# A list scheduler's assumed durations, set to fits of the durations in a trace

## Chip, cores and metric

The kernel runs on one core of one Trainium2 chip. The metric is the device time of one execution in microseconds. The median of three runs before the change is 1693.6 us (1693.36 to 1693.68).

## What is computed

Two transformer blocks on 512 tokens of width 1024, in fp32. The first block has two mixers side by side (gated linear attention with 4 heads, "GLA", and latent softmax attention with 8 heads, "MLA"), an MLP of width 4096 and an embedding gate. The second is a pool mixer, a gated convolutional FFN of width 2816, chunk attention with 16 heads, and a second such FFN:

```
h = h + concat(gla(n), mla(n)) @ w_out              # stage mix
h = h + square(relu(norm(h) @ w_up)) @ w_down       # stage mlp
h = h + (p @ w_proj) * sigmoid(norm(h) @ w_gate+b)  # stage ple
x = x + pool_mixer(norm(x))                         # stage pool
x = x + (silu(conv(n @ Wg)) * (n @ Wv)) @ Wo        # stage ffn0
x = x + chunk_attention(norm(x)) @ w_o              # stage att
x = x + (silu(conv(n @ Wg)) * (n @ Wv)) @ Wo        # stage ffn1
```

## The kernel before, in words

Every large product is split into a high and a low part, and each pair of tiles gets three matmuls (`mm3`, L328). Weights come in units of 128 x 1024. Each unit is split by ScalarE (`wh`) and by VectorE or GpSimd (`wl`, L257). TensorE takes the 512 tokens as moving operand, or 256 columns in the token-major products (`tm`, L359: `pgv`, `paq`). The outputs live in 8 PSUM banks.

**What sets the order of the work.** The instructions of each engine run in the order in which the program issues them, and this order is not written out by hand. The kernel is a set of Python generators ("tasks"). Each yields, before a step, the tiles that the step reads, or a condition. `drive` (L197) picks the next step while the program is built: among the tasks whose tiles are expected to be ready when TensorE gets there, it takes the one with the lowest priority number; if none is ready, the one that is ready first. The main task has the number 9. It issues the large products ("filler" below). The attention and GLA chains have 2 to 4 and evacuations have 0, so they go first whenever they are judged ready:

```
now = self.pace.free["tensor"] + self.SLACK
best = min([(t[0], t) for at, t in able if at <= now], ...)
```

What is "expected" comes from `Pace` (L60). For each issued instruction `note` (L82) works out a cost. The instruction starts when its engine is free and its tiles are ready. The engine is then free again after the cost, and the output counts as ready 0.08 us after that (2.0 us for a DMA). So one number is at once how long the engine is held and how long the result takes. A step that is judged ready too early makes its engine wait with all that is queued behind it. One that is judged ready too late is queued behind work that did not have to be ahead of it.

The same clock decides between engines. `first` (L297) takes the engine that is expected to be done first: VectorE or GpSimd for products and differences in SBUF (`sub`, `mul`, L304 and L309), VectorE or ScalarE for scalings and copies (`scaled`, `copy`, L314 and L321), where `TURN` adds 1.0 us to one side.

In the mix stage the filler is `pg`, `pgv` and then `pw` (the output product). `pw` takes GLA's first two heads and MLA's first two pairs, then GLA's last two heads, and last MLA's pairs 2 and 3, for which all of MLA must be done. MLA goes through 4 pairs of heads with 4 tiles of queries each, one tile at a time (`AHEAD_M` = 1, 1). A tile is: scores `msc`; VectorE memsets, maximum and product `msc`, `mnm`, `mnb`; ScalarE exponentials with a sum, `prob`; VectorE reciprocal `mrs` and scaling `prob`; TensorE transposes `mt`; copies `probT`; TensorE `mo` into a divided array (64 columns). Chunk attention has 8 pairs in the same form (`asc`, `sbias`, `anb`, `prob`, `at`, `probT`, `ao`), with up to 4 tiles under way; its `asc` with `aql` uses 64 rows of the array. Its filler is `paq`, then `pw` in three parts, the last of which needs every pair. At the end of a stage the residual `x` is added up, and the next stage's `xsh`, `xsl`, squares `sq` and their sums `pst` are made.

Of the kernel before, what the change touches and what calls it, by code (L numbers as in the profile page):

```python
# [10 lines left out]
F32R = mybir.dt.float32r  # L11
I32 = mybir.dt.int32
AF = mybir.ActivationFunctionType
OP = mybir.AluOpType
AX = mybir.AxisListType

P = 128
# [42 lines left out]
class Pace:  # L60
    """An estimate of when the engines get to each instruction, from which the order of issue is chosen."""

    def __init__(self):
        self.free = dict.fromkeys(("tensor", "vector", "scalar", "gpsimd", "sync"), 0.0)
        self.ready, self.open, self.banks, self.table = {}, {}, [0.0] * 8, None
        self.mine, self.step = set(), 0

    def allot(self, tile):
        """a bank goes to a tile: the one that was given up first"""
        self.ready[tile.tensor.name] = self.banks.pop(0)  # L70
        self.open[tile.tensor.name] = (0, 0.0)

    def give_up(self, n):
        """the n banks that were read last are given up"""
        for name in sorted(self.open, key=lambda k: self.open[k][0])[-n:]:
            self.banks.append(self.open.pop(name)[1])
# [5 lines left out]
    def note(self, engine, op, args, kw):  # L82
        aps = [x for x in list(args) + list(kw.values()) if hasattr(x, "tensor") and hasattr(x, "free_size")]
        outs = aps[:1] + ([kw["accum_out"]] if kw.get("accum_out") is not None else [])
        ins = aps[1:] + (aps[:1] if op == "copy_predicated" else [])
        n, m = self.size(outs[0]), max([self.size(x) for x in ins], default=0)
        if engine == "tensor":
            if op == "transpose":
                cost = 0.109
            elif ins[0].dtype == F32R:  # L90
                cost = max(0.054, n / 2400)
            else:
                cost = max(0.214, n / 600) * (0.5 if outs[0].shape[0] == 64 else 1)
        elif engine == "vector":
            fast = op in ("tensor_copy", "tensor_scalar") and all(x.space == "SB" or "SB" in str(x.space) for x in aps)
            cost = 0.068 + (m if op == "tensor_reduce" else n) / (1920 if fast else 960)
            if any(n > 1 and x.free_size() == 1 for x in ins):
                cost += 0.063
        elif engine == "scalar":
            cost = 0.09 + n / 1190 + (0.093 if len(outs) > 1 or hasattr(kw.get("scale"), "tensor") else 0)  # L100
        elif engine == "gpsimd":
            cost = 0.23 + 0.165 * n if kw.get("op") == OP.pow else 0.1 + n / (350 if ins else 1400)
        else:
            cost = outs[0].shape[0] * n * 4 / 360e3
        if engine == "scalar":
            f = next((str(x) for x in args if isinstance(x, mybir.ActivationFunctionType)), "")
            if any(f.endswith(x) for x in ("Exp", "Ln", "Sin", "Silu", "Sigmoid")) and f != self.table:
                self.table = f
                cost += 1.28
        needs = ins + [x for x in outs if x.tensor.name not in self.mine or engine != "tensor"]  # L110
        start = max([self.free[engine]] + [self.ready.get(x.tensor.name, 0.0) for x in needs])
        if engine == "tensor":
            self.mine.add(outs[0].tensor.name)
        self.free[engine] = start + cost
        self.step += 1
        if engine != "tensor":
            for x in ins:
                if x.tensor.name in self.open:
                    self.open[x.tensor.name] = (self.step, start + cost + 0.08)
        for x in outs:  # L120
            self.ready[x.tensor.name] = start + cost + (2.0 if engine == "sync" else 0.08)
# [22 lines left out]
class Norm:  # L144
    """the residual times a norm's gain, split, and the reciprocal rms: a column per token tile, and broadcast"""
# [15 lines left out]
class Block:  # L161
# [22 lines left out]
    # order of issue ---------------------------------------------------------  # L184
    def spawn(self, gen, prio):
        """gen yields before each step what the step reads, or a condition it waits for"""
# [34 lines left out]
    # memory -------------------------------------------------------------------  # L221
# [24 lines left out]
    # weights --------------------------------------------------------------------  # L246
# [10 lines left out]
    def split_unit(self):  # L257
        """the next unit's high and low parts"""
# [24 lines left out]
    def unit(self, *shape):  # L283
        """the next unit, as (high, low) of [128, blocks, columns]; its split is issued when it is used up"""
# [12 lines left out]
    def first(self, aps, **cost):  # L297
        """the engine that is expected to be done first; cost: fixed part, per element, handicap"""
# [5 lines left out]
    def sub(self, out, a, b):  # L304
        """a - b, all in SBUF"""
        e = self.first((out, a, b), vector=(0.07, 1 / 960, 0), gpsimd=(0.1, 1 / 430, self.HELP))
        getattr(self.nc, e).tensor_sub(out, a, b)

    def mul(self, out, a, b):  # L309
        """a * b, all in SBUF"""  # L310
        e = self.first((out, a, b), vector=(0.07, 1 / 960, 0), gpsimd=(0.1, 1 / 430, self.HELP))
        getattr(self.nc, e).tensor_mul(out, a, b)

    def scaled(self, out, src, col):  # L314
        """src times a column, in SBUF"""
        if self.first((out, src, col), vector=(0.13, 1 / 1920, 0), scalar=(0.18, 1 / 1190, self.TURN)) == "vector":
# [4 lines left out]
    def copy(self, out, ps):  # L321
        """out of PSUM"""
        if self.first((out, ps), vector=(0.07, 1 / 960, self.TURN), scalar=(0.09, 1 / 1190, 0)) == "vector":
# [27 lines left out]
    def fm(self, ps, unit, acts, at=0, n=None):  # L351
        """feature-major product: the unit's blocks from `at` on stationary, acts[k] moving"""
# [6 lines left out]
    def tm(self, xs, out):  # L359
        """token-major product of 256 columns; out: two banks of two token tiles"""  # L360
# [14 lines left out]
    # norms of the residual ------------------------------------------------------  # L375
# [61 lines left out]
    # first block: both mixers ---------------------------------------------------  # L437
# [9 lines left out]
    def mix_start(self, norm):  # L447
        """the first loads in the order of need"""
# [28 lines left out]
        # constants of this part  # L477
# [65 lines left out]
    def latent(self, i, ps, norm):  # L543
        """evacuates latent i (keys and values, queries, queries) or the low-rank gate and rotary key"""
# [37 lines left out]
    def mla_weights(self):  # L582
        """the up-projections' weights, split: [(hi, lo)] of 512 (keys, values) and 384 columns"""
# [7 lines left out]
    def rotate(self, out, src, tab, j, n):  # L591
        """out, src: [P, n, 32]; the two halves of a rotary pair, gains folded into the tables"""
# [13 lines left out]
    def mla(self, norm):  # L606
# [5 lines left out]
        # the shared rotary key  # L612
# [17 lines left out]
        # keys and values  # L630
# [90 lines left out]
    def attend(self, pr, vals, scale, bias, name, ahead, scored):  # L721
        """heads[pr][head]: the products that make up a head's scores; adds the pair's output, transposed and split"""
# [82 lines left out]
    def gla_inputs(self, norm, ft):  # L805
        """queries and keys of two heads, feature-major"""
# [22 lines left out]
    def gla_values(self, norm, ft):  # L829
        """values and output gate of two heads: tiles of two token tiles by two heads"""  # L830
# [19 lines left out]
    def gla_gate(self):  # L850
        """the logarithms of the decays, split: tiles of two token tiles"""
# [31 lines left out]
        # queries of a level, one head's beside the other's with zeros between  # L883
# [5 lines left out]
    def gla(self, ft):  # L889
        """two heads"""  # L890
# [81 lines left out]
        def finish(b, ou):  # L972
            """two token tiles: the heads' norm, the gate, and the result transposed and split"""
# [84 lines left out]
    def part_out(self, acts, after=lambda m: None):  # L1058
        """adds the product of some K tiles with their rows of an output matrix"""
# [61 lines left out]
    # first block: MLP -------------------------------------------------------------  # L1121
# [23 lines left out]
    def product(self, norm, name, finish):  # L1145
        """one feature tile of a product with the normed residual"""
# [8 lines left out]
    def products(self, norm, name, finish, first):  # L1155
        """feature tiles of products with the normed residual; the first two side by side while the residual comes in"""
# [46 lines left out]
    # first block: per-layer embedding gate ------------------------------------------  # L1203
# [14 lines left out]
    def project(self):  # L1218
        """the embedding's projection, which needs nothing of the residual"""
# [43 lines left out]
    # second block: pool mixer ---------------------------------------------------------  # L1263
# [70 lines left out]
    # second block: gated convolutional FFN ----------------------------------------------  # L1334
# [50 lines left out]
    # second block: chunk attention --------------------------------------------------------  # L1385
# [8 lines left out]
    def attention(self, norm, after):  # L1394
# [6 lines left out]
        def heads():  # L1401
            for pr in range(8):
# [3 lines left out]
                # a head's product with both parts of the keys in one pass: the high part of its queries is there twice  # L1406
# [94 lines left out]
    # -----------------------------------------------------------------------------------  # L1501
# [60 lines left out]
def pack_fm(w, kts):  # L1562
    """[K, M] -> one unit per M tile: [128, len(kts) * 128]"""
# [5 lines left out]
def pack_tm(w, n=512, ks=2):  # L1569
    """[K, N] -> units of ks K tiles by n columns, K within a column group first"""  # L1570
# [5 lines left out]
def pack_parts(w, parts):  # L1576
    """[K, M] -> for each group of K tiles, units of 8 blocks: M tiles, and the K tiles of each"""
# [120 lines left out]
```

## Time and profile before

| | |
|---|---|
| median of the runs | 1693.6 us (1693.36 to 1693.68) |
| span of the profiled execution | 1689.6 us |
| between the span and the median, what lies around the span | 4.0 us |
| TensorE busy | 98% of the span |
| VectorE, ScalarE, GpSimd busy | 60%, 43%, 11% |
| mean granted TensorE clock | 0.998 |

The profiled execution has no time of its own beside its span; the three runs lie within 0.32 us, so it is set beside their median. "Busy" is the union of the instructions' intervals. An interval of a matmul goes on after the next one has started, so a busy TensorE is not one that starts matmuls at its full rate. All engine instructions carry line L133 (the wrapper that notes each one), so they are told apart by the names of their tiles.

### The profile page before, as it was taken

What the parts mean: (1) busy time and instruction counts of PE and PEld (TensorE: products, weight loads), DVE (VectorE), ACT (ScalarE), POOL (GpSimd) and SP (SyncE); (2) the same over time, 40 slices, a digit from 0 to 9 for tenths busy, and PEclk for the clock granted to TensorE, in tenths of its full rate; (3) what the DMA queues carried; (4) which work ended last, traced back from release to release, by engine and by line L of the source; (5) the groups of instructions that cost most, each with busy time, mean ns of one, the idle gap of its engine ahead of it and who ended that gap; (6) DMA issues with size and microseconds to landing.
All of it is one profiled execution on the core that took longest, in us unless ns stands there. A gap on an engine that the chain in (4) does not pass through costs nothing.

```text
span 1689.6 us, 22483 instructions
## 1 busy us (share of the span) xinstructions
PE 1660.7 (98%) x8696; PEld 1389.8 (82%) x8696; DVE 1007.0 (60%) x1889; ACT 728.3 (43%) x1422; POOL 184.3 (11%) x190
## 2 busy tenths in 40 slices
PE   8999999999999999999999999999999999999999
PEld 6878777888888888888888888989987788888887
DVE  6986867443444357766644645375768776644642
ACT  6745445432333254643332324365656543322321
POOL 3431302000000012200000001121222100000000
PEclk9999999999999999999999999999999999999999
DMA  6102032333323333233333233312221233333332
GB/s 215 62 26 64 24 115 75 100 100 94 105 88 113 92 90 108 65 109 91 99 100 89 94 100 102 116 64 88 68 96 51 76 100 99 100 102 98 90 100 73
DMA packets 47501, 153.73 MB, mean 91 GB/s; under 512 B 5521, under 2 KB 7458, under 8 KB 47394
## 3 DMA queue, kind: packets, MB, share of 16 engines
q1 hardware_dynamic: 47394, 152.30, 29.2%
q8 instruction: 68, 1.11, 0.3%
q14 instruction: 39, 0.32, 0.1%
HBM read 150.18 MB, written 2.10 MB: 90 GB/s over the span
## 4 chain that ended last, share of the span: by engine, by line
PE 87%; DVE 8%; ACT 3%; issue 1%; DMA 0%; SPq 0%; POOL 0%; DVEq 0%; ACTq 0%
PE pf L133 27%; PE pdn L133 24%; PE pup L133 10%; PE paq L133 7%; PE pw L133 3%; PE pgv L133 2%; PE pgt L133 2%; DVE wl L133 1%; PE pl L133 1%; PE ao L133 1%; PE at L133 1%; ACT aqh L133 1%; DVE xsl L133 1%; PE pg L133 1%; DVE x L133 1%
## 5 line engine op out<-in xcount | busy, mean ns | idle before, releaser
L133 ACT ACTIVATE wh<-ws 128x512 fp32r<-128x512 f32 (+1 forms) x536 | 302.7, 614 | 254.1 <-PE pdn L133 213.9
L133 DVE TENSOR_TENSOR wl<-ws,wh 128x512 fp32r<-128x512 f32 (+1 forms) x508 | 343.8, 717 | 110.6 <-ACT wh L133 110.3
L133 PE MATMUL pf<-xsl,wh 128*128 128x512 f32 x704 | 274.7, 390 | 1.4 <-DVE xsl L133 1.2
L133 PE MATMUL pf<-xsh,wh 128*128 128x512 f32 x704 | 275.4, 391 | 0.0
L133 PE MATMUL pf<-xsh,wl 128*128 128x512 f32 x704 | 274.2, 390 | 0.0
L133 DVE TENSOR_TENSOR x<-x,pdn 128x512 f32<-128x512 f32 (+1 forms) x81 | 55.1, 681 | 219.2 <-PE pdn L133 219.2
L133 PEld LDWEIGHTS pf<-xsl,wh 128*128 128x128 f32 x704 | 132.2, 188 | 31.2 <-DVE xsl L133 3.6
L133 PEld LDWEIGHTS pf<-xsh,wh 128*128 128x128 f32 x704 | 132.2, 188 | 28.2 <-issue 0.5
L133 PEld LDWEIGHTS pf<-xsh,wl 128*128 128x128 f32 x704 | 132.2, 188 | 27.0
L133 PE MATMUL pdn<-yl,wh 128*128 128x512 f32 x352 | 137.1, 389 | 0.0
L133 PE MATMUL pdn<-yh,wl 128*128 128x512 f32 x352 | 137.1, 389 | 0.0
L133 PE MATMUL pdn<-yh,wh 128*128 128x512 f32 x352 | 137.0, 389 | 0.0
L133 POOL TENSOR_TENSOR sq<-sq 128x512 f32<-128x512 f32 x37 | 51.9, 1403 | 744.5 <-ACT sq L133 743.7
L133 PE MATMUL paq<-wh,xsh 128*128 128x256 f32 x384 | 113.2, 295 | 0.8 <-DVE aql L133 0.4
L133 PE MATMUL paq<-wh,xsl 128*128 128x256 f32 x384 | 109.4, 285 | 0.0
L133 PE MATMUL paq<-wl,xsh 128*128 128x256 f32 x384 | 109.4, 285 | 0.0
L133 PE MATMUL pup<-xsl,wh 128*128 128x512 f32 x256 | 99.8, 390 | 0.4 <-DVE xsl L133 0.4
L133 PE MATMUL pup<-xsh,wh 128*128 128x512 f32 x256 | 100.2, 391 | 0.0
L133 PE MATMUL pup<-xsh,wl 128*128 128x512 f32 x256 | 99.7, 389 | 0.0
L133 PE MATMUL pdn<-hl,wh 128*128 128x512 f32 x256 | 99.7, 389 | 0.0
L133 PE MATMUL pdn<-hh,wl 128*128 128x512 f32 x256 | 99.7, 389 | 0.0
L133 PE MATMUL pdn<-hh,wh 128*128 128x512 f32 x256 | 99.7, 389 | 0.0
(292 smaller groups left out, 3092.3 us busy)
## 6 DMA issues: line engine op xcount, KB each, us to landing
ws<-in_w_fg SPq DMA_DIRECT2D x44, 512.0 KB, 3.6
ws<-in_w_fv SPq DMA_DIRECT2D x44, 512.0 KB, 3.6
ws<-in_w_up SPq DMA_DIRECT2D x32, 512.0 KB, 3.6
ws<-in_w_down SPq DMA_DIRECT2D x32, 512.0 KB, 3.6
ws<-in_w_fo SPq DMA_DIRECT2D x32, 448.0 KB, 3.2
ws<-in_w_fo SPq DMA_DIRECT2D x16, 512.0 KB, 3.6
ws<-in_w_out SPq DMA_DIRECT2D x8, 512.0 KB, 3.6
ws<-in_w_gate SPq DMA_DIRECT2D x8, 512.0 KB, 3.7
```

What stands on the lines that cost most here:

```text
L133: return call(*args, **kw)
```

## The change

The costs in `Pace.note` and the engines' prices in `sub`, `mul`, `scaled` and `copy` are replaced. `Pace` gets one more state, `mode`, the part of the array that the last matmul used; a matmul in another mode is charged 0.1 us more (coming from the whole array) or 0.2 us more (coming from a divided one), and one with 64 rows or 64 columns costs half. The kernel's instructions, their sizes and data, the tasks, their priorities and the other constants stay as they are; docstrings and comments are dropped.

```diff
         if engine == "tensor":
+            rows, columns = ins[0].shape[0], self.size(ins[0])
             if op == "transpose":
-                cost = 0.109
-            elif ins[0].dtype == F32R:
-                cost = max(0.054, n / 2400)
+                cost, mode = 0.109, (P, P)
             else:
-                cost = max(0.214, n / 600) * (0.5 if outs[0].shape[0] == 64 else 1)
+                mode = tuple(next(t for t in (32, 64, P) if x <= t) for x in (rows, columns))
+                cost = n / 2400 + 0.0135 if ins[0].dtype == F32R else max(0.224, n / 600 + 0.005)
+                if 64 in mode:
+                    cost *= 0.5
+            if mode != self.mode:
+                cost += 0.1 if self.mode == (P, P) else 0.2
+                self.mode = mode
         elif engine == "vector":
             fast = op in ("tensor_copy", "tensor_scalar") and all(...)
-            cost = 0.068 + (m if op == "tensor_reduce" else n) / (1920 if fast else 960)
+            cost = 0.152 + (m if op == "tensor_reduce" else n) / (1920 if fast else 960)
             if any(n > 1 and x.free_size() == 1 for x in ins):
-                cost += 0.063
+                cost += 0.065
         elif engine == "scalar":
-            cost = 0.09 + n / 1190 + (0.093 if len(outs) > 1 or hasattr(kw.get("scale"), "tensor") else 0)
+            cost = 0.165 + n / 1190 + (0.19 if len(outs) > 1 else 0)
+            cost += 0.1 * sum(hasattr(kw.get(x), "tensor") for x in ("scale", "bias"))
         elif engine == "gpsimd":
-            cost = 0.23 + 0.165 * n if kw.get("op") == OP.pow else 0.1 + n / (350 if ins else 1400)
+            cost = 0.38 + 0.157 * n if kw.get("op") == OP.pow else 0.175 + n / (459 if ins else 1400)
...
     def sub(self, out, a, b):          # and mul
-        e = self.first((out, a, b), vector=(0.07, 1 / 960, 0), gpsimd=(0.1, 1 / 430, self.HELP))
+        e = self.first((out, a, b), vector=(0.152, 1 / 960, 0), gpsimd=(0.175, 1 / 459, self.HELP))
...
-        if self.first((out, src, col), vector=(0.13, 1 / 1920, 0), scalar=(0.18, 1 / 1190, self.TURN)) == "vector":
+        if self.first((out, src, col), vector=(0.217, 1 / 1920, 0), scalar=(0.265, 1 / 1190, self.TURN)) == "vector":
...
-        if self.first((out, ps), vector=(0.07, 1 / 960, self.TURN), scalar=(0.09, 1 / 1190, 0)) == "vector":
+        if self.first((out, ps), vector=(0.152, 1 / 960, self.TURN), scalar=(0.165, 1 / 1190, 0)) == "vector":
```

## Rows read from the trace of the kernel before

**Rows 1.** The page: span, engines, the chain that ended last by engine.

```profile
span 1689.6 us, 22483 instructions
PE 1660.7 (98%) x8696; PEld 1389.8 (82%) x8696; DVE 1007.0 (60%) x1889; ACT 728.3 (43%) x1422; POOL 184.3 (11%) x190
...
PE 87%; DVE 8%; ACT 3%; issue 1%; DMA 0%; SPq 0%; POOL 0%; DVEq 0%; ACTq 0%
```

**Rows 2.** Busy time by stretch: engine busy us (x instructions), then clock, DMA share, GB/s.

```profile
72.00:203.00 131.00, 124.41 (x901) 105.21 (x900) 102.00 (x304) 65.50 (x156) 43.21 (x70) 1.00 0.14 41
203.00:253.00 50.00, 49.54 (x271) 38.00 (x269) 34.38 (x90) 27.12 (x64) 2.46 (x2) 1.00 0.33 106
253.00:276.00 23.00, 20.65 (x91) 16.20 (x90) 20.26 (x25) 13.24 (x23) 7.59 (x5) 1.00 0.22 68
276.00:618.00 342.00, 342.00 (x1510) 283.05 (x1510) 154.22 (x237) 119.41 (x207) 7.54 (x6) 1.00 0.33 98
...
714.00:1058.00 344.00, 344.00 (x1520) 285.00 (x1519) 196.87 (x293) 124.38 (x213) 9.27 (x8) 1.00 0.33 99
1058.00:1311.00 253.00, 248.75 (x1972) 223.73 (x1972) 168.45 (x365) 144.48 (x348) 51.66 (x48) 0.99 0.24 78
```

**Rows 3.** The chain of waits in order of time: start us, us, what.

```profile
238.18 1.06 PE msc L133 x4
239.24 4.78 PE pw L133 x21
244.02 0.44 PE mt L133 x4
...
251.88 0.17 PE mt L133
...
862.17 43.52 PE pdn L133 x192
```

**Rows 4.** Waits of TensorE from 40 to 254 us: sum, times, longest.

```profile
PE mt L133 <- DVE prob L133: 1.7, 2, 1.5
PE pe L133 <- DVE sct L133: 1.6, 3, 0.8
PE po L133 <- DVE msc L133: 1.1, 2, 0.6
```

**Rows 5.** Waits of TensorE from 254 us to the end, same columns.

```profile
PE pst L133 <- DVE sq L133: 3.2, 3, 1.7
PE at L133 <- DVE prob L133: 2.5, 2, 1.5
```

**Rows 6.** Timeline of VectorE, 238 to 252 us: one MLA tile's instructions.

```profile
240.21 1.28 DVE L133 TENSOR_TENSOR x<-x,pw 128x512 f32<-128x512 f32 x2
242.02 0.69 DVE L133 TENSOR_TENSOR x<-x,pw 128x512 f32<-128x512 f32 x1 [0.53 <-PE pw L133]
242.62 0.16 DVE L133 RECIPROCAL mrs<-msu 128x2 f32<-128x2 f32 x1
242.82 0.62 DVE L133 TENSOR_SCALAR prob<-prob,mrs 128x256 f32<-128x256 f32 x2
```

**Rows 7.** Timeline of ScalarE in the same tile.

```profile
240.79 0.19 ACT L133 ACTIVATION_READ_ACCUMULATOR prob<-msc,mnb,qs 128x1 f32 x1
240.88 0.56 ACT L133 ACTIVATE prob<-msc,mnb,qs 128x256 f32<-128x256 f32 x1
241.33 0.20 ACT L133 ACTIVATION_READ_ACCUMULATOR prob<-msc,mnb,qs 128x1 f32 x1
```

**Rows 8.** Timeline of TensorE, 1307 to 1312 us: the last tiles of chunk attention.

```profile
1310.56 0.40 PE L133 MATMUL pw<-omh,wl 128*128 128x512 f32 x1
1310.89 0.44 PE L133 MATMUL ao<-probT,aqkv 128*64 128x128 f32 x4
```

**Rows 9.** VectorE and GpSimd lines, 0 to 276 us: count, busy us, mean ns.

```profile
L133 DVE TENSOR_TENSOR wl<-ws,wh 128x512 fp32r<-128x512 f32 (+1 forms) x52 | 40.1, 812 | 15.9 <-ACT wh L133 15.7
L133 POOL TENSOR_TENSOR wl<-ws,wh 128x512 fp32r<-128x512 f32 x4 | 5.2, 1320 | 6.2 <-ACT wh L133 6.1
```

More of the change, by code (lines that the diff above doesn't have):

```diff
@@ L65, in __init__ @@
         self.ready, self.open, self.banks, self.table = {}, {}, [0.0] * 8, None
-        self.mine, self.step = set(), 0
+        self.mine, self.step, self.mode = set(), 0, (P, P)
     def allot(self, tile):
@@ L304, in sub @@
     def sub(self, out, a, b):
-        e = self.first((out, a, b), vector=(0.07, 1 / 960, 0), gpsimd=(0.1, 1 / 430, self.HELP))
+        e = self.first((out, a, b), vector=(0.152, 1 / 960, 0), gpsimd=(0.175, 1 / 459, self.HELP))
         getattr(self.nc, e).tensor_sub(out, a, b)
     def mul(self, out, a, b):
-        e = self.first((out, a, b), vector=(0.07, 1 / 960, 0), gpsimd=(0.1, 1 / 430, self.HELP))
+        e = self.first((out, a, b), vector=(0.152, 1 / 960, 0), gpsimd=(0.175, 1 / 459, self.HELP))
         getattr(self.nc, e).tensor_mul(out, a, b)
     def scaled(self, out, src, col):
-        if self.first((out, src, col), vector=(0.13, 1 / 1920, 0), scalar=(0.18, 1 / 1190, self.TURN)) == "vector":
+        if self.first((out, src, col), vector=(0.217, 1 / 1920, 0), scalar=(0.265, 1 / 1190, self.TURN)) == "vector":
             self.nc.vector.tensor_scalar(out, src, col, None, op0=OP.mult)
```

## Prediction

> **What bounds the kernel now.** I read the page first: TensorE is busy for 98% of the span and carries 87% of the chain that ended last [rows 1]. The reader is to see that little is left to gain by order alone. The table of stretches says where. In 276 to 618 us and 714 to 1058 us TensorE is busy for the whole stretch [rows 2], and the chain of waits shows the rate there: 192 matmuls of 512 columns in 43.52 us [rows 3], 0.2267 us each. No order of the other engines changes that, so these stretches (and ffn1 after 1334 us, of the same make) count as zero. TensorE has idle time only where attention and GLA steps are mixed into the filler: 131.00 - 124.41 = 6.6 us in 72 to 203, 0.5 in 203 to 253, 2.3 in 253 to 276, and 253.00 - 248.75 = 4.3 in 1058 to 1311 [rows 2]. Together that is 13.7 us. The lists of TensorE's waits say for whom: nearly all for VectorE, on a chain's step that was issued before its data were there (`prob`, `sct`, `msc`, and `sq` ahead of the sums `pst`) [rows 4, 5]. While it waits, filler stands behind it in the queue. So the planner of before is too optimistic at these places, and its costs can move at most these idle times, and whatever a new order adds.
>
> **How far the old costs are off.** TensorE: n/2400 gives 0.2133 us for 512 columns, the trace 0.2267 [rows 3]. The planner's TensorE runs 6% fast, and the new cost gives 0.2268. VectorE: one add of 512 elements lasts 0.69 us, but two back to back take 1.28 us, so the second starts 0.59 us after the first [rows 6]. The old cost 0.068 + 512/960 = 0.601 is the time for which the engine is held; with the 0.08 us that follow, the result comes after 0.68 us, which is the duration. The new cost is the duration, 0.685, so engine and result are each late, by 0.084 us. ScalarE: an exponential of 256 columns with its sum holds the engine 0.45 + 0.09 = 0.54 us (starts at 240.79, 240.88 and 241.33) [rows 7]. The old cost is 0.09 + 0.215 + 0.093 = 0.40, the new one 0.165 + 0.215 + 0.19 + 0.2 = 0.77. So TensorE's fit becomes right, VectorE's goes from right to 14% too long for 512 elements (and to twice as long for the smallest), and ScalarE's goes from too short to too long.
>
> **The change part by part.**
>
> *Instructions.* None is added or removed, the DMAs too are the same; only their order on each engine and the choice between engines move. The dividing term saves no switch: `drive` chooses by priority and readiness, not by cost. It only makes the planner's TensorE later at `mo`, `ao` and `aql`. Zero by itself.
>
> *TensorE's waits.* For an MLA tile of 256 columns I add the planner's costs from the last score to the first transpose (2 memsets, 2 maxima, a product, 2 exponentials, a reciprocal, 2 scalings, with the 0.08 us at each hand-over). Old: 0.27 + 0.67 + 0.15 + 0.88 + 0.15 + 0.61 + 0.08 = 2.8 us. New: 0.44 + 0.84 + 0.23 + 1.62 + 0.23 + 0.78 + 0.08 = 4.2 us. So the transposes are placed 1.4 us later by the planner's clock, less what its slower TensorE takes back: a tile's period is about 9 us, 6% of that is 0.5 us. About 0.9 us net, four of the new filler matmuls more between scores and transposes. Of the listed waits three are longer than 1.2 us (1.5, 1.5, 1.7) [rows 4, 5]; the others would be covered by 0.9 us of filler, and these shortened. The sums `pst` come after VectorE's `xsl` and `sq`, all dearer by 0.084 us, and have the next stage's filler to stand behind. Bounds: nothing is gained, if the new order makes as many waits as it takes away; all 13.7 us go but for 0.7 (the first products that wait for `xsl` or `oml` and have nothing else to run), and each wait gives back 0.39 - 0.23 = 0.16 us of a pipeline that ran empty, some 16 times 2.6 us: 15.6. I take **-8**, near the middle, because 0.9 us covers most of the single waits, while VectorE's queue has a new order too and will be late at places of its own.
>
> *VectorE's own blocks.* In the tile at 240 us the reciprocal stood behind an add of `x` that waited 0.53 us for `pw` [rows 6]; the planner had thought TensorE further on. The right matmul cost takes this away. It is part of what the chains gain, and I count it in the next term.
>
> *The ends of the chains.* MLA's 16 tiles come one after another. The last transposes are at 251.88 us, and the filler before the last part of `pw` ran until then [rows 3]; in chunk attention the last `ao` follows three filler matmuls [rows 8]. At both ends chain and filler run out together, so a later chain shows as an idle TensorE. With 0.9 us a tile, 16 tiles are 14 us late against the filler, which is 1.5 tiles of 9 us; each of them left without filler costs at most the 4.78 us between its scores and transposes and some 1.4 us between those and `mo` [rows 3], 9 us in all. It costs nothing if the chain's lost waits (7.1 us of idle time until 253 us) and blocks bring it forward as much. Chunk attention has four tiles under way, which hides lateness until the last pair: 0 to 4 us. I take **+4** of these 13 for both, since the last tiles are the smallest and have an empty VectorE before them (34.38 of 50 us) [rows 2].
>
> *Choice of engine.* The price gap of a 512-element difference between GpSimd and VectorE falls from 1.29 - 0.60 = 0.69 to 1.29 - 0.685 = 0.61 us, and the planner's VectorE is further behind, so more `wl` go to GpSimd than the 4 beside 52 until 276 us [rows 9]. That relieves VectorE by 0.6 us each; but `wl` takes 812 ns there on average [rows 9] against 690 for an add of the same size [rows 6], so something slows it, and more work on GpSimd may slow it more. Bounds -2 and +3, taken as **0**.
>
> Sum: -8 + 4 + 0 = -4. The profiled execution has span 1689.6 us [rows 1], and 4.0 us lie around it to the median 1693.6, to which the runs keep within 0.2 us. I predict **1689.6 us**.
>
> **The rivals.** About 0.2%, 3.4 us, is what a measurement of this kernel can tell from no change.
>
> *Slower: the planner's VectorE is full.* From 72 to 203 us VectorE has 304 instructions and is busy for 102.0 us [rows 2]. At 0.084 us more each the planner's VectorE needs up to 127.5 of 131 us. A queue that is nearly full grows, and every chain step behind it is placed late, though the real engine is free. Then the filler is used up with more than two tiles of queries to come, and TensorE idles for the chains at the ends: +9 in mix, +4 in attention, and of the waits only 3 us are saved: +10, 1703.6 us. For it: the start-to-start times above, and ends without margin. Against it: the tile at 238 us took 4.8 us from scores to transposes [rows 3], more than the 4.2 of the new costs. It decides from two tiles left over. The Trainium skill speaks for this rival ("Perfetto Trace Analysis", section "Per-engine timelines"): the interval that the profiler shows for a VectorE or ScalarE instruction ends with the acknowledgement of its last write, and the next one can begin before that. By that rule durations are the wrong thing to hold an engine for, and the time would be this rival's; the trace agrees, with 0.59 us to the next start beside 0.69.
>
> *No change.* New waits replace the old ones, or the ends take back what the waits give: 1690.2 to 1697.0, about 1693. For it: at both ends chain and filler already meet, so the chains themselves, not the waits, may set the length.
>
> *More is gained.* All waits go and the ends keep up: -15.6 + 2, about 1680. For it: the waits sit where the planner's error for TensorE accumulates; against it: VectorE's queue becomes less true, not more.
>
> **How the numbers follow.** Forecast (-3.5 to -9) 0.34, more gained 0.10, no change 0.23, slower 0.33. So faster 0.44, same 0.23, slower 0.33. Range: below, the forecast's waits almost all gone, 1682; above, the slower rival with GpSimd's +3, 1706. Outside lie some of "more gained" and of a worse tail, 0.2 together. The faster cases alone would span 1678 to 1690.
>
> **What would show it.** Right: the dense stretches keep 43.52 us for 192 matmuls; TensorE's waits for `prob`, `sct` and `sq` from 40 us on shrink to about half; the last `mo` before the last part of `pw` comes earlier than 252 us; more `wl` on GpSimd. Wrong: TensorE waits for `prob` or `probT` several times in a row just before the last part of `pw`, in mix or in attention, with no filler between (the slower rival); or a list of waits as long as before at other steps (no change). The forecast falls if the idle time of 72 to 276 us does not shrink.

## The result: 1.0% slower, and the profile after

The changed kernel takes **1711.3 us** (median of four runs, 1708.1 to 1712.0) against 1693.5 us for the kernel before (four runs, 1691.7 to 1693.7): a ratio of 1.0100, with a 95% interval of 1.0085 to 1.0116. The forecast was 1689.6 us, the range ended at 1706. It went the way of the slower rival, and further than that rival's 1703.6.

The page of the changed kernel, lines as in [rows 1]:

```profile
span 1709.0 us, 22482 instructions
PE 1662.7 (97%) x8696; PEld 1390.6 (81%) x8696; DVE 1005.2 (59%) x1852; ACT 730.6 (43%) x1423; POOL 205.5 (12%) x226
...
PE 87%; DVE 9%; ACT 3%; issue 1%; DMA 0%; SPq 0%; DVEq 0%; ACTq 0%
```

The spans differ by 19.4 us. TensorE is busy for only 2.0 us more (1662.7 against 1660.7), so 17.4 us are idle time: 46.3 us instead of 28.9. Where it arose is read from busy time by stretch, with both kernels cut at the same steps: the first down product `pdn` of the MLP, the first and the last `paq` of chunk attention, the end. The columns are those of [rows 2]. First the kernel before, then the changed one:

```profile
0.00:356.20 356.20, 338.10 (x1915) 276.74 (x1916) 254.28 (x644) 189.29 (x389) 83.17 (x104) 1.00 0.27 85
356.20:1057.80 701.60, 700.00 (x3165) 581.10 (x3164) 376.87 (x564) 265.58 (x464) 38.78 (x30) 1.00 0.32 97
1057.80:1257.70 199.90, 197.10 (x1665) 184.22 (x1665) 123.43 (x272) 113.92 (x274) 39.81 (x39) 0.99 0.26 83
1257.70:1689.60 431.90, 425.46 (x1957) 347.76 (x1955) 252.46 (x409) 159.53 (x297) 22.60 (x18) 1.00 0.29 89
```

```profile
0.00:366.90 366.90, 336.42 (x1914) 277.70 (x1915) 252.16 (x612) 188.59 (x389) 99.74 (x136) 0.99 0.25 83
366.90:1071.80 704.90, 700.77 (x3165) 581.19 (x3164) 374.65 (x561) 267.14 (x466) 39.23 (x31) 1.00 0.31 97
1071.80:1277.30 205.50, 199.61 (x1664) 183.55 (x1664) 125.29 (x273) 115.29 (x273) 40.36 (x39) 0.99 0.25 80
1277.30:1709.00 431.70, 425.94 (x1957) 348.12 (x1955) 253.14 (x406) 159.61 (x296) 26.17 (x20) 1.00 0.29 89
```

The loss is 10.7 us up to the MLP's first down product, 3.3 in the middle, 5.6 in `paq`, and -0.2 after that. In the first stretch TensorE's idle time grew from 18.1 to 30.5 us, though VectorE has 2.1 us less to do. TensorE's longest waits, as in [rows 4, 5] but over the whole span:

```profile
PE pl L139 <- ACT wh L139: 9.5, 1, 9.5
PE mt L139 <- DVE prob L139: 5.6, 3, 3.0
PE at L139 <- DVE prob L139: 4.6, 5, 1.1
PE po L139 <- DVE sct L139: 3.9, 2, 2.6
PE pf L139 <- DVE xsl L139: 3.1, 2, 2.3
PE plv L139 <- DVE gqt L139: 2.3, 1, 2.3
```

The first is the wait for the first weights. It had 7.8 us before, and the runs below that keep the changed kernel's order have 8.1 and 8.3, so more than 1 of the 10.7 us is scatter of the start and not the order's. Of the others, `mt` for `prob` had 1.7 us before, `at` for `prob` 2.5. Only the wait of the sums `pst` for `sq` shrank as forecast, from 3.2 to 0.4 us.

**MLA's chain starts late.** All its scores, first in the kernel before, then in the changed one (shortest, median and longest duration in ns, then the first and the last start in us):

```profile
L133 PE MATMUL msc<-hd x64: 273/484/595, 75.2 to 247.5; 96*128 96x512 f32 x16, 96*128 96x384 f32 x16, 96*128 96x256 f32 x16, 96*128 96x128 f32 x16
L139 PE MATMUL msc<-hd x64: 273/484/676, 90.8 to 260.4; 96*128 96x512 f32 x16, 96*128 96x384 f32 x16, 96*128 96x256 f32 x16, 96*128 96x128 f32 x16
```

The first scores come 15.6 us later, and the last group of `mo` 11.6 us later (263.96 for 252.39). From the one to the other the changed kernel takes 4 us less, so the chain is late from its start and not by a little more in each tile.

**The end of mix.** The chain of waits of the changed kernel, 242 to 260 us (start, length, what):

```profile
242.45 1.49 PE msc L139 x4
243.94 7.50 PE pw L139 x33
251.44 0.66 PE mt L139 x6
...
253.60 1.07 PE msc L139 x4
```

And TensorE's timeline right behind it:

```profile
257.63 0.76 PE L139 MATMUL mt<-ident,prob 128*128 128x128 f32 x4 [2.97 <-DVE prob L139]
...
263.12 0.69 PE L139 MATMUL mt<-ident,prob 128*128 128x128 f32 x2 [2.33 <-DVE prob L139]
263.96 0.90 PE L139 MATMUL mo<-probT,vm 128*64 128x128 f32 x4 [0.15 <-ACT probT L139]
264.79 0.80 PE L139 MATMUL pw<-omh,wh 128*128 128x512 f32 x1
```

The filler between scores and transposes of the last three tiles was, in the kernel before:

```profile
230.56 4.79 PE pw L133 x21
...
239.24 4.78 PE pw L133 x21
...
247.78 4.10 PE pw L133 x18
```

Here the first of these three tiles got 33, three more stand ahead of its `mo`, and then the filler was used up: the last two tiles have none, and TensorE waits 2.97 and 2.33 us. The last part of `pw` starts at 264.79 instead of 253.0 us. VectorE's timeline shows what stood ahead of the tile with 33:

```profile
245.21 1.87 DVE L139 TENSOR_TENSOR x<-x,pw 128x512 f32<-128x512 f32 x3
247.30 1.29 DVE L139 TENSOR_TENSOR wl<-ws,wh 128x512 fp32r<-128x512 f32 x2 [0.21 <-ACT wh L139]
248.51 0.68 DVE L139 TENSOR_TENSOR x<-x,pw 128x512 f32<-128x512 f32 x1
249.11 0.16 DVE L139 RECIPROCAL mrs<-msu 128x2 f32<-128x2 f32 x1
```

The row sums were there at 246.75 us, but the reciprocal stands in VectorE's order behind four additions and two `wl`. In the program its step is picked only when the planner expects the sums, so it presumably expected ScalarE's exponentials later than they were; the planner's clock is in no trace, so this is not shown.

**The clock.** Behind the first of those two waits TensorE lost some of its clock. The same view by stretch, around them:

```profile
253.00:259.00 6.00, 2.88 (x24) 1.76 (x22) 2.32 (x9) 1.92 (x6) 0.00 (x0) 1.00 0.00 0
259.00:270.00 11.00, 8.52 (x29) 6.21 (x30) 4.70 (x13) 4.36 (x11) 0.00 (x0) 0.53 0.14 44
```

And for two single microseconds of it:

```profile
258.00:259.00 1.00, 0.85 (x7) 0.48 (x8) 0.00 (x0) 0.71 (x2) 0.00 (x0) 1.00 0.00 0
259.00:260.00 1.00, 1.00 (x8) 0.71 (x9) 0.00 (x0) 0.00 (x0) 0.00 (x0) 0.64 0.00 0
```

TensorE was busy for 2.88 of 6 us, and in the 11 us that follow the mean granted clock is 0.53, mostly the lower level of 1.2 GHz. It fell between 259 and 260 us, behind the first wait and ahead of the second. The 48 matmuls of the last part of `pw` took 13.0 us (264.8 to 277.8, from the first start to the last). At the rate of [rows 3] that would be 10.7, so the clock cost some 2.3 us there. Before, the same part took 11.4 us at full clock, some 0.7 of it lost around a wait for `oml`.

### The profile page after: what moved, and what is told of

Its sections match the earlier page's. It is cut to its first block, busy times and chain, and to the rows that moved or that the text cites. A ratio compares the mean times of both kernels' runs of the same rounds, so it can differ in the third digit from the quotient of the medians.

```text
span 1709.0 us, 22482 instructions
## 1 busy us (share of the span) xinstructions
PE 1662.7 (97%) x8696; PEld 1390.6 (81%) x8696; DVE 1005.2 (59%) x1852; ACT 730.6 (43%) x1423; POOL 205.5 (12%) x226
## 4 chain that ended last, share of the span: by engine, by line
PE 87%; DVE 9%; ACT 3%; issue 1%; DMA 0%; SPq 0%; DVEq 0%; ACTq 0%
PE pf L139 27%; PE pdn L139 24%; PE pup L139 10%; PE paq L139 6%; PE pw L139 4%; PE pgt L139 3%; PE pgv L139 2%; PE pl L139 1%; PE ao L139 1%; DVE gqt L139 1%; PE at L139 1%; PE msc L139 1%; ACT aqh L139 1%; DVE prob L139 1%; DVE wl L139 1%
## 5 line engine op out<-in xcount | busy, mean ns | idle before, releaser
L139 DVE TENSOR_TENSOR wl<-ws,wh 128x512 fp32r<-128x512 f32 (+1 forms) x497 | 335.5, 715 | 129.2 <-ACT wh L139 129.1
```

The lines of the kernel that those rows point to most:

```text
L139: return call(*args, **kw)
```

## Experiments

Ratios are to runs of the kernel before on the same chip in the same session, with 95% intervals.

### One part of the change at a time

The kernel before, with TensorE's costs alone:

```diff
+rows, columns = ins[0].shape[0], self.size(ins[0])
...
+    cost = n / 2400 + 0.0135 if ins[0].dtype == F32R else ...
...
+if mode != self.mode: ...
```

> Only TensorE's costs of the change, with the term for a divided array; VectorE, ScalarE, GpSimd and the prices as before. Theory A (the harm is in charging a VectorE or ScalarE instruction its whole duration as time for which the engine is held): no slower than before, 1685 to 1695 us, MLA's first scores near 75 us as before. Theory B (TensorE's new costs or the term for the divided array move the filler wrongly): most of the 18 us are here, 1703 to 1713. Theory C (any new order loses some microseconds against the old one, whatever its costs): 1696 to 1705.

1715.5 us, ratio 1.0132 (1.0114 to 1.0151). So the one fit that became true [rows 3], together with the term for the divided array, loses by itself, and more than any of the three theories had. TensorE waits for `sq` twice for 3.3 us and once 3.6 us for `xsl`.

VectorE's costs alone:

```diff
-cost = 0.068 + ...
+cost = 0.152 + ...
```

> Only VectorE's costs of the change in the planner's clock. Theory A: VectorE is overbooked in the planner, MLA's chain starts late (first scores after 85 us instead of 75) and its last tiles have no filler: 1700 to 1712 us. Theory B: within 3 us of before. Theory C: 1696 to 1705.

1711.4 us, 1.0105 (1.0085 to 1.0126): as much as the whole change, and where Theory A had it. MLA's first scores come at 89.6 us, as late as in the whole change, and the last tile has no filler. The longest wait is one `po` for `mrs`, 4.8 us.

```profile
L133 PE MATMUL msc<-hd x64: 272/484/736, 89.6 to 266.2; 96*128 96x512 f32 x16, 96*128 96x384 f32 x16, 96*128 96x256 f32 x16, 96*128 96x128 f32 x16
```

ScalarE's costs alone:

```diff
-cost = 0.09 + n / 1190 + (0.093 if ...)
+cost = 0.165 + n / 1190 + (0.19 if len(outs) > 1 else 0)
+cost += 0.1 * sum(...)
```

> Only ScalarE's costs of the change in the planner's clock. Theory A: MLA's chain starts as before (75 us), since VectorE and TensorE set that, but each tile's exponentials are placed late, the filler is gone before the last tiles, and TensorE waits for them at the end of mix: 1697 to 1708 us. Theory B: within 3 us of before. Theory C: 1696 to 1705.

1729.9 us, 1.0228 (1.0204 to 1.0252), the worst part. What Theory A described came, with the first scores at 78.4 us, but the time is 22 us above its range. TensorE's timeline shows the end of mix without filler for four tiles, not two:

```profile
266.64 1.97 PE L134 MATMUL mt<-ident,prob 128*128 128x128 f32 x8 [2.93 <-DVE prob L134]
...
277.63 1.51 PE L134 MATMUL mt<-ident,prob 128*128 128x128 f32 x6 [3.50 <-DVE prob L134]
...
286.05 0.96 PE L134 MATMUL mt<-ident,prob 128*128 128x128 f32 x4 [2.96 <-DVE prob L134]
...
292.16 0.43 PE L134 MATMUL mt<-ident,prob 128*128 128x128 f32 x2 [2.42 <-DVE prob L134]
```

GpSimd's costs and the prices in `first` alone:

```diff
-cost = ... 0.1 + n / (350 if ins else 1400)
+cost = ... 0.175 + n / (459 if ins else 1400)
...
-vector=(0.07, 1 / 960, 0), gpsimd=(0.1, 1 / 430, self.HELP)
+vector=(0.152, 1 / 960, 0), gpsimd=(0.175, 1 / 459, self.HELP)
```

> Only GpSimd's costs and the prices between engines (sub, mul, scaled, copy). Theory A: GpSimd's fit is nearer to its start-to-start times than the old one, so no harm, 1688 to 1696 us. Theory B: within 3 us of before. Theory C: 1696 to 1705.

1708.4 us, 1.0095 (1.0071 to 1.0120), above all three theories. Each part alone loses 15 to 37 us, 92 in sum where the whole loses 18. So the parts don't add up, and no part is the cause by itself. MLA's late start does belong to one part: with TensorE's, ScalarE's or GpSimd's costs alone the first scores come at 77.9 to 78.6 us, with VectorE's alone at 89.6. But an end of mix without filler is not the only way to lose: with TensorE's or GpSimd's costs alone each of the last three tiles has 15 to 21 filler matmuls behind its scores, and in the profiled executions the first `pdn` still comes at 370.3 and 372.3 us instead of 356.2.

### Is any other order worse?

Three shifts of the old costs that mean next to nothing, and one repair of the change: its costs for TensorE and GpSimd, VectorE and ScalarE held from start to start, their results handed over later (this last diff is against the changed kernel).

```diff
-SLACK = -0.1
+SLACK = -0.15
```

> The kernel before with every old cost; only the constant SLACK of the planner is -0.15 us instead of -0.1, a change that makes no cost truer or less true. Theory C (the old order is one picked among many that the old costs and constants can give, and any other order loses): 1700 to 1712 us. Theory A (only wrong holding times lose): within 4 us of before.

```diff
-cost = max(0.054, n / 2400)
+cost = max(0.054, n / 2388)
```

> The kernel before, with the F32R matmul's cost n/2388 in place of n/2400, half a percent more and so a little truer. Theory C: 1700 to 1712 us. Theory A: within 4 us of before.

```diff
-cost = 0.068 + ...
+cost = 0.070 + ...
```

> The kernel before, with VectorE's fixed cost 0.070 us in place of 0.068. Theory C: 1700 to 1712 us. Theory A: within 4 us of before.

```diff
-cost = 0.152 + ...
+cost = 0.068 + ...
...
-cost = 0.165 + n / 1190 + (0.19 ...)
-cost += 0.1 * sum(...)
+cost = 0.09 + n / 1190 + (0.093 ...)
+cost += 0.07 * sum(...)
...
-self.ready[...] = start + cost + (2.0 if engine == "sync" else 0.08)
+self.ready[...] = start + cost + dict(sync=2.0, vector=0.124, scalar=0.135).get(engine, 0.08)
```

> TensorE's and GpSimd's costs and the prices of the change; VectorE and ScalarE are held for the times from one start to the next (the old costs, with the sum at 0.093 us and each column operand of ScalarE at 0.07 us), and their results come 0.124 and 0.135 us after that. This is the planner whose clock is nearest to the trace. Theory A: it beats the change by 10 us or more and is at or below before, 1680 to 1695 us. Theory C: like any new order, 1700 to 1712 us.

Slack: 1693.8 us, 1.0003 (0.9992 to 1.0015). Half a percent on the matmuls: 1701.3, 1.0057 (1.0035 to 1.0079). Two ns on VectorE: 1697.9, 1.0042 (1.0028 to 1.0057). Start-to-start holding: 1705.2, 1.0068 (1.0048 to 1.0089). So 2 ns in one cost can move the time by 0.4%, by nothing but another order, and the repair gains 6 us on the change, but not on the kernel before. Theory A, that only wrong holding times lose, is out: the repair lies 10 us above its range, and half a percent more on the matmuls loses too, though it is nearer to the trace. Theory C, that any other order loses, has the time of these two runs; the shift of the slack lost nothing, and the one of 2 ns lies between the theories.

### Can the change be repaired, and what do shifts of it give?

In the changed kernel: less work for GpSimd, less slack, more slack, 2 ns.

```diff
-HELP, TURN = 0.0, 1.0
+HELP, TURN = 1.0, 1.0
```

> The change with HELP = 1.0 in place of 0: GpSimd gets a difference or product only where the planner has VectorE over 1 us later. Theory E (work moved to GpSimd stretches VectorE's instructions beside it, and so delays the chains): the time falls, 1697 to 1706 us. Theory F (the chains are late because the planner's VectorE is overbooked): VectorE is booked even more, the chains come later still, 1711 to 1725 us.

```diff
-SLACK = -0.1
+SLACK = -0.15
```

> The change with SLACK = -0.15 in place of -0.1, which makes no cost truer or less true. If the 18 us come from the costs, it stays near the change: 1706 to 1716 us. If they come from the picked order of before alone, it may land anywhere between 1695 and 1725 us.

```diff
-SLACK = -0.1
+SLACK = 0.9
```

> The change with SLACK = +0.9: a step counts as ready 1 us earlier against TensorE than in the change. Theory F: about what the new costs put on a tile is taken back, MLA's last tile is done long before the filler ends, TensorE's waits at the end of mix go, 1695 to 1704 us. If the late chains were not the cause: 1708 to 1718 us, or slower by waits of TensorE on steps that are issued too early.

```diff
-cost = 0.152 + ...
+cost = 0.154 + ...
```

> The change with VectorE's fixed cost 0.154 us in place of 0.152. As with the changed SLACK: 1706 to 1716 us if the level belongs to the costs, anywhere between 1695 and 1725 us if orders differ by chance alone.

All are slower than the change: 1731.5 us (1.0213; 1.0195 to 1.0231), 1725.2 (1.0174; 1.0157 to 1.0190), 1733.3 (1.0221; 1.0203 to 1.0240) and 1730.6 (1.0206; 1.0184 to 1.0227). The repairs (less GpSimd, chains let in 1 us earlier) failed. Their times lie above the ranges expected of them, of which the highest ended at 1725 us; only the run with more slack had "or slower" beside its range. The two shifts that mean nothing add 14 and 19 us (13 and 18 by the ratios), so the change itself was a good draw among the orders of its costs that ran.

### Carried on, or lost stage by stage?

The new costs in mix alone, and after mix alone (`self.new` chooses the set, and flips when a stage's generator ends):

```diff
+    self.pace.new = False      # starts True
```

> The new costs hold for the first stage (mix) alone; from its end on the old ones are used. The order on TensorE is that of the changed kernel for its first 1064 rows. Theory G (each stage loses by its own order): mix ends as in the changed kernel, so the first down product starts at 366 to 368 us, and from there on the kernel before repeats itself: its 1329.3 us from that point, so 1700 to 1707 us in all. Theory H (the loss is made in mix and carried on, whatever the later costs): 1709 to 1713 us.

```diff
+    self.pace.new = True       # starts False
```

> The old costs hold in mix, the new ones from its end on. The order on TensorE is that of the kernel before for its first 1053 rows. Theory G: the first down product starts at 356 us as before, and the later stages lose 6 to 10 us by their own order (chunk attention most), 1699 to 1705 us. Theory H: 1692 to 1696 us.

1705.0 us, 1.0061 (1.0044 to 1.0079), and 1702.4, 1.0053 (1.0033 to 1.0074). Above the kernel before (1695.3 in that session) that is 9.7 and 7.1 us, 16.8 in sum, beside the 17.8 of the whole change: Theory G (each stage loses by its own order). Busy time by stretch, cut at the same steps, shows it without the median. New costs in mix alone:

```profile
0.00:367.80 367.80, 339.85 (x1914) 281.36 (x1915) 251.86 (x613) 188.95 (x389) 98.16 (x135) 0.97 0.25 83
367.80:1069.50 701.70, 700.10 (x3165) 581.03 (x3164) 376.65 (x564) 265.38 (x464) 38.93 (x30) 1.00 0.31 97
1069.50:1267.60 198.10, 195.48 (x1664) 182.60 (x1663) 123.30 (x272) 113.91 (x274) 39.97 (x38) 1.00 0.26 83
```

New costs after mix alone:

```profile
0.00:360.10 360.10, 341.45 (x1915) 278.99 (x1916) 254.08 (x644) 189.45 (x389) 83.16 (x104) 0.99 0.26 84
360.10:1065.00 704.90, 700.78 (x3166) 581.24 (x3165) 374.65 (x561) 267.07 (x466) 39.27 (x31) 1.00 0.31 97
1065.00:1269.00 204.00, 198.10 (x1665) 182.12 (x1664) 125.17 (x273) 115.43 (x273) 40.35 (x39) 1.00 0.25 80
```

Each stretch has the length that belongs to its costs: 701.7 or 704.9, 198 or 204. The first one also shows the noise: 360.1 us here with the order that took 356.2 before. Differences of less than 4 us in a single profile of mix are not read as effects.

### Are durations as holding times what raises the level?

Two shifts of the planner with start-to-start holding (the last diff of the second group), in the same way as above:

```diff
-SLACK = -0.1
+SLACK = -0.15
```

> The planner that holds VectorE and ScalarE from start to start and hands the result over later (1705.2 us), with its slack moved from -0.1 to -0.15 us, which has no meaning of its own. Theory L (durations used as holding times raise the level of the whole family): small shifts of a planner with right holding times stay between 1698 and 1708 us, below all three shifts of the changed kernel (1725, 1731, 1733). Theory S (any order other than the one in place is a draw from a wide lot, whatever the costs): this run and the next differ from 1705 by over 8 us, one of them above 1713.

```diff
-cost = 0.068 + ...
+cost = 0.070 + ...
```

> The same planner with 2 ns more for each VectorE instruction. Theory L: 1698 to 1708 us. Theory S: over 8 us from 1705, or the run with the other slack is. In both kernels the last score tile of mix has no filler behind it by the order, so TensorE is expected to wait for its prob once, 2 to 3 us, at the end of mix.

1713.3 us, 1.0109 (1.0091 to 1.0127), and 1704.1, 1.0056 (1.0041 to 1.0071). Neither theory comes out clean: the first run lies above Theory L's 1708 and over 8 us from 1705, as Theory S wants; the second lies where Theory L has it, with the one wait of 2.3 us for `prob` at the end of mix. Each set of costs with its shifts of the slack by 0.05 us and of VectorE by 2 ns (medians in us, from different sessions, in which the kernel before had 1691.8 to 1695.8):

| planner | as is | slack | 2 ns |
|---|---|---|---|
| old costs | 1693.5 | 1693.8 | 1697.9 |
| start-to-start holding | 1705.2 | 1713.3 | 1704.1 |
| durations (the change) | 1711.3 | 1725.2 | 1730.6 |

Inside a row the orders scatter by 4 to 19 us. The means of the last two rows are 1707.5 and 1722.4. That points to some 15 us (14 by the ratios) that durations as holding times cost, but with three orders in each row, whose ranges overlap, it is not shown. The parts of the change speak against a level that hangs on this alone: TensorE's costs with the old holding times took 1715.5 us. Clearer is where MLA starts: first scores at 74.8 to 76.2 us with the old costs and their shifts, 83.6 to 84.5 in the second row, 89.7 to 90.8 in the third. Between the means of the first two rows lie another 12.5 us, and what makes the old costs that good is not settled by these runs. One rival was hardly tried: the planner's other constants are those that went with the old costs, and the new ones ran with only one other `HELP` and two other values of the slack.

### What does GpSimd's share cost?

These two keep the changed kernel's order on every engine. The planner still books the work on GpSimd, and VectorE does it: the first four `wl` that GpSimd got, and then all 50 `gqt` that it got.

```diff
+if e == "gpsimd" and self.early <= 4:
+    self.pace.note(e, "tensor_sub", (out, a, b), {})
+    self.nc.vector.real.tensor_sub(out, a, b)
+    return
```

> The changed kernel with its order and its planner untouched; only the first four weight differences that it gives to GpSimd (40.96 to 46.6 us) are done by VectorE, at their places in the order, behind the rotary tables. Theory P (GpSimd's work beside them stretches VectorE's copies, and that holds the start of the chains back): the gm copies take 0.9 instead of 3.08 us, gkc 0.15 instead of 1.24, the four small ropew 0.65 instead of 1.57; two of the four wl come ahead of glow (1.3 us), so glow starts at 47.5 to 48.5 instead of 50.65 us and pkr at 48.5 to 49.5 instead of 51.4; mix ends 1 to 3 us earlier, the whole run 1707 to 1710 us. Rival Q (the stretch has another cause, such as the waits of those copies): gm keeps 3 us, four wl are added, glow starts at 52 us or later and the run takes 1712 to 1716 us.

```diff
+if e == "gpsimd" and self.pace.size(out) == 64:
+    self.pace.note(e, "tensor_mul", (out, a, b), {})
+    self.nc.vector.real.tensor_mul(out, a, b)
+    return
```

> The changed kernel with its order and its planner untouched; all 50 small products gqt (64 x 64) that it gives to GpSimd are done by VectorE at their places in the order. Theory P: GpSimd loses 16.8 us of work, VectorE gets 50 more at 0.21 us or less, some 7 to 10 us, and gives up stretched ones (62 at a mean of 434 ns, the longest 3.7 us); TensorE's wait plv for gqt of 2.3 us at 147 us goes, and the run takes 1707 to 1711 us. Rival R (relief of VectorE is worth having even so): VectorE's queue is late by the added 7 to 10 us in 90 to 195 us, TensorE waits longer for sct and prob there, 1713 to 1722 us.

First run: 1712.3 us, 1.0110 (1.0094 to 1.0127). Half of Theory P holds. VectorE's timeline of the changed kernel, and then of this run:

```profile
41.08 3.08 DVE L139 CAST gm<-gmf 128x512 fp32r<-128x512 f32 x3
44.09 1.24 DVE L139 TENSOR_TENSOR gkc<-cols 96x1 f32<-96x1 f32 x1
...
45.45 1.57 DVE L139 TENSOR_SCALAR ropew<-inv,pf 128x16 f32<-128x16 f32 x4
```

```profile
42.25 0.89 DVE L139 CAST gm<-gmf 128x512 fp32r<-128x512 f32 x3
43.06 0.15 DVE L139 TENSOR_TENSOR gkc<-cols 96x1 f32<-96x1 f32 x1
...
43.32 0.65 DVE L139 TENSOR_SCALAR ropew<-inv,pf 128x16 f32<-128x16 f32 x4
```

The copies take 0.89 us without GpSimd beside them and 3.08 with it. But `glow` starts only 1.8 us earlier (48.82 for 50.65), `pkr` 0.8, and the time is that of Rival Q, the same as the change's. MLA's first scores stay at 90.1 us (90.8 in the change), so trading the stretched copies for four `wl` on VectorE gives nothing, and what an earlier start of MLA would give was not tried.

Second run: 1718.6 us, 1.0145 (1.0132 to 1.0159): Rival R. The first `pdn` comes at 375.9 us, against 366.9 and 368.3 in the other two runs of this order. So GpSimd's share of `gqt`, all 50 of them, is worth 7 to 9 us in the changed kernel's order, although it slows VectorE where they meet.

## Why the prediction was wrong, point by point

**Dense stretches: right.** 287 to 629 us and 727 to 1071 us are busy throughout, as in [rows 2], and 192 matmuls still take 43.52 us.

**The -8 for TensorE's waits: this step failed.** The idle time was forecast to shrink and grew by 17.4 us. The waits for `prob`, `sct` and `sq`, which were to halve, went from 10.0 to 16.8 us. I had read the mean shift (0.9 us a tile, four filler matmuls more between scores and transposes) as cover for waits whose places are known from [rows 4, 5]. That shift did not come: counted in the timelines over MLA's 16 tiles, 360 filler matmuls stand between a tile's last score and its first transpose, where 483 stood before, and the chain is late by its start instead. A new set of costs doesn't shift an order, it makes another one, with waits at other places: `po` for `sct`, 2.6 us at 117 us; `plv` for `gqt`, 2.3 at 154; `mt` for `prob`, 3.0 at 258. The kernel before had 13.7 us of idle time in the mixed stretches, so there was little to win and much to lose. The single parts and the shifts agree: of the 17 other orders that ran, the change's own among them, none beat the old one, and one equalled it. The bounds of this term reached from 0 to -15.6; that it could be a loss was left out.

**VectorE's own blocks: wrong.** I expected the right matmul cost to take such blocks away. The reciprocal at 249.11 us, 2.4 us after its sums, is a longer one, behind two `wl` and four additions.

**The ends, +4: the outcome in mix foreseen, its size too small, its source another.** Two tiles are without filler, each waiting 2 to 3 us; 5.3 us of waits. But the prediction made the chain late by 0.9 us in each tile, and it was late by 15.6 us at its first scores. What was not in the sum is the clock: at 1.2 GHz the part behind the two tiles took some 2.3 us more. In attention the loss was not at the end (431.9 and 431.7 us) but inside `paq`, 4 to 6 us: TensorE waits there five times for `prob` instead of once. Why the new order has these waits is open.

**Choice of engine, 0: right about the loss, for another reason.** GpSimd did get more (`wl` x10 for x4 and `gqt` x50 for x27 until 287 us). It slows VectorE, as feared, but giving the four early `wl` back changed nothing, and giving the 50 `gqt` back cost 7 to 9 us. In this order it isn't where the time went.

**The slower rival** named the direction, the reason (VectorE and ScalarE held for their durations) and the point at which it decides (two tiles left over). Its +9 for mix and +4 for attention are near what the stretches show (10.7 and 5.6, of which the runs with split costs confirm 9.7 and 4 to 6). The 3 us of waits that it took off didn't come, and the 3.3 us in the middle (`pf` for `xsl`, `pu` for `xsh`) were not seen. Its picture of a planner that has VectorE full, so that chain steps are placed late, fits MLA's start: with VectorE's costs alone the first scores are as late as in the change. That the late start makes the 10.7 us was not tried by itself. That holding for durations costs time is what the table above points to, and does not show. The section of the Trainium skill that the prediction weighed ("Perfetto Trace Analysis", section "Per-engine timelines") lets the next instruction begin before the shown end of the one ahead of it. The trace agrees, with 0.59 us between starts beside 0.69 shown [rows 6]. What that is worth in time these runs leave open, so the direction of the result is no proof of it.

**The test that the prediction set itself:** "The forecast falls if the idle time of 72 to 276 us does not shrink." It grew from 9.4 to 17.8 us, and the last `mo` came at 264 us instead of before 252. Of the other signs, more `wl` on GpSimd came, and the waits in a row before the last part of `pw` are those of the slower rival.

## What to carry to other kernels

A list scheduler's costs are not measurements to be made true one at a time: each edit is a new order, so time a few meaningless shifts beside it, and trust a difference only when it is larger than theirs. An engine's holding time is the distance from one start to the next (0.59 us for an addition of 512 elements here), and the profile's duration (0.69 us) is longer, so one number can't stand for both. Where a chain and its filler end together, look in the new order at where the chain starts and how much filler is left for the last tiles before believing any sum of waits.

## What the runs showed of the hardware

**VectorE and GpSimd get in each other's way.** Three copies in SBUF took 3.08 us beside GpSimd's `wl` and 0.89 without, and one of the products `gqt` (64 x 64, 0.21 us at the least) took 3.68 us beside GpSimd's work at 148 to 154 us. The Trainium skill ("SBUF — State Buffer", section "Who interferes with whom") says that VectorE in a two-port mode, or with two inputs in SBUF while GpSimd reads there, shares a pair of ports with GpSimd, which goes to one instruction at a time while the other waits. The run that took GpSimd's `wl` away agrees for the copies (0.89 us), and the one that took its `gqt` away for the product (1.25 us at the most); which of the two waits more often was not tried.

**A wait of TensorE can cost twice.** In the changed kernel TensorE was busy for 2.88 of the 6 us up to 259 us, with a wait of 2.97 us among them, and then its granted clock fell to 1.2 GHz until about 270 us. Not every such wait does this: after those of 2.61 us at 117 us and 2.34 us at 154 us the granted clock stayed at 1.00. In the profiled execution of the run with ScalarE's costs alone, with four tiles without filler, the mean granted clock of the whole span is 0.982, against 0.998 before, and TensorE's busy time rose from 1660.7 to 1685.0 us for the same matmuls.
